# Embedding inputs of a two-block network: loaded and split ahead of the mixer instead of behind it

## The chip, the cores and the metric

One core of one Trainium2 chip runs the whole program, launched once. The metric is the device time in microseconds, the median of 3 runs. Engines: PE is TensorE (matmuls), DVE is VectorE, ACT is ScalarE, POOL is GpSimd, SP is SyncE (here it issues the DMAs of the weights). All arithmetic is float32; matmuls are made of three passes over halves, as told below.

## The reference

Two blocks over 256 tokens of width 1024. The first block is attention (differential and latent) and an FFN. The second has two layers, and the change lies in these. Layer `i` computes, with `rmsnorm` before and after each part:

```
for i in range(2):
    h = h + 0.5 * rmsnorm(ffn(rmsnorm(h)))                 # FFN (i, 0)
    m = retention(rmsnorm(h)) if i == 0 else stick_breaking(rmsnorm(h))
    h = h + rmsnorm(m)                                     # the mixer
    h = h + 0.5 * rmsnorm(ffn(rmsnorm(h)))                 # FFN (i, 1)
    gate = sigmoid(rmsnorm(h) @ ple_w_gate[i])
    e = p[i] @ ple_w_proj[i]                               # the embedding
    h = h + rmsnorm(gate * e)
```

`p[i]` is an input of 256 x 256, `ple_w_proj[i]` one of 256 x 1024. So `e` depends on nothing that is computed before it.

## The kernel before

**Three passes.** Each float32 operand is split into a high half, rounded to the matmul's format (`hi`), and the rest (`lo = x - hi`). A product is `hi*hi + hi*lo + lo*hi`, three matmuls into one PSUM bank (`mm3`). A split is one operation of ACT (the rounding copy) and one of DVE (the subtraction): L180 and L181 for weights (`w_hi`, `w_lo`), L275 and L276 for other tiles (`split`), L408 and L409 for the features of a stage (`x_hi`, `x_lo`).

**Weights.** All weights lie in one array in the order of use. `chunk` loads up to 2048 columns of it by a DMA on SP into one of 3 raw buffers, and splits them in pieces of 512 columns into tiles of the pools `hip` (tag "a") and `lop` (tag "b"), 12 buffers each. Buffers of a tag are given out in the order of the program.

**Stages.** In a stage by tokens (`tokens`), the 256 tokens are two halves `b`, and weights are taken in groups of k-tiles; within a group first half 0, then half 1. At the end of an FFN or mixer `end_stage` runs the output projection (behind a mixer only its second 512 columns, with a last group of 8 k-tiles of 512 columns), and `residual` normalizes each half and adds it to `h`: two squares on ACT with a sum (L377), products on DVE (L387), a power on POOL (L303), and the addition on DVE (L394). `features` prepares a half of `h` for the next stage: 8 transposes on PE (L404) into two PSUM tiles of the pool `psa` (4 banks), 8 `x_hi` and 8 `x_lo`, two more squares for the scale `R`. The squares write to scratch tiles of tag "sq" in the pool `tmp`, 2 buffers, which nobody reads.

**The embedding.** `embed` is called behind the mixer. It opens with a DMA from POOL of `p[i]`, transposed, into `pt` (L1184), in a pool of its own that lies where the mixer's tiles were. It splits `pt` into `pe_a` and `pe_b`, a buffer each of `hip` and `lop` (L1185 to L1189). Then 24 matmuls of 512 columns through `tokens`, with one chunk of weights (4 pieces), fill the four banks of `psa`, and four copies on ACT write `e` (L1194). `ple` uses `e` some 200 us later.

**Order.** The order of each engine's instructions is made by a planner when the program is built. It gives an engine, of the instructions whose inputs and buffers are ready by its own cost model, the one that stands first in the program; `urgent` moves `residual` and `features` up by 100 places. Each engine then works through its list in order, and waits at an instruction whose inputs are late. Tiles of pools that are open at different times share memory, and a tile waits until those that lay there before it are done with.

Of the kernel before, what the change touches and what calls it, by code (L numbers as in the profile page):

```python
# [10 lines left out]
F32 = mybir.dt.float32  # L11
F32R = mybir.dt.float32r
# [6 lines left out]
P = 128  # L19
T = 256  # L20
# [16 lines left out]
SUB = 512  # L37
# [100 lines left out]
class Build:  # L138
# [1038 lines left out]
                self.end_stage("sb_w_out_2", (0,), oT, KT, row, first=first)  # L1177


    def embed(self, emb, i, e):  # L1180

        nc = self.nc
        pt = emb.tile([P, 2, T], F32, name="pt")
        nc.gpsimd.dma_start(pt, self.aps["pT"][:, i * 2 * T : (i + 1) * 2 * T].rearrange("p (k t) -> p k t", k=2))  # L1184
        hi, lo = [  # L1185
            pool.tile([P, SUB], F32R, name=f"pe_{tag}", tag=tag).rearrange("p (k t) -> p k t", k=2)
            for pool, tag in ((self.hip, "a"), (self.lop, "b"))
        ]
        self.split(pt, hi, lo)  # L1189
        parts = [("ple_w_proj_2", (i,), range(j * 512, (j + 1) * 512)) for j in range(2)]  # L1190
        banks = self.banks(self.psa, "a")
        for b, _ in self.tokens(parts, (hi, lo), 2, banks, [[0, 1]]):
            for j in range(2):
                nc.scalar.copy(e[:, b, j * 512 : (j + 1) * 512], banks[b][j])  # L1194
# [30 lines left out]
    def run(self):  # L1225
        tc = self.tc
        self.setup()
        g2 = lambda i, n: self.vec(V_G2 + (i * 8 + n) * 8, 8)
        row = lambda i, n: R_G2 + 4 * i + n // 2
        stage = self.first()  # L1230
        with tc.tile_pool(name="big0", bufs=1) as self.big:
            self.ffn(*stage, ("w_ffn_gate", "w_ffn_up", "w_ffn_down"), (0,), R_FFN, 1.0)
        names = ("ffn_w_gate_2", "ffn_w_up_2", "ffn_w_down_2")
        out = self.aps["out"].rearrange("p (b d) -> p b d", b=2)
        for i in range(2):
            with tc.tile_pool(name=f"big{i}a", bufs=1) as self.big:
                self.ffn(*self.next_stage(g2(i, 0)), names, (i, 0), row(i, 1), 4.0)
            mixer = self.stick if i else self.retention
            mixer(*self.next_stage(g2(i, 2)), row(i, 3))
            with tc.tile_pool(name=f"emb{i}", bufs=1) as emb:  # L1240
                e = emb.tile([P, 2, D], F32, name="e")
                self.embed(emb, i, e)
                with tc.tile_pool(name=f"big{i}b", bufs=1) as self.big:
                    self.ffn(*self.next_stage(g2(i, 4)), names, (i, 1), row(i, 5), 4.0)
                self.ple(i, *self.next_stage(g2(i, 6), 4.0), e, row(i, 7), out if i else None)
        assert self.at == WCOLS * P, (self.at, WCOLS * P)
# [67 lines left out]
```

## Time and profile before

| What | Value |
|---|---|
| time, median of 3 runs | 1652.93 us (1652.63 to 1652.97) |
| the profiled execution | 1655.98 us, span 1654.2 us |
| PE busy | 1617.8 us, 98% of the span |
| DVE, ACT, POOL busy | 65%, 54%, 4% |
| mean granted clock of PE | 0.991 of full speed |
| HBM read | 284.75 MB, 173 GB/s over the span |

Times in the profile count from the start of the span. Busy is the time in which an engine works on an instruction; matmuls overlap, so the start of one to the start of the next tells their pace better than a duration. In a timeline a bracket behind a row is the time that the engine stood idle before it, and what ended that. The granted clock is the share of TensorE's full clock that it got: 1.00 is 2.4 GHz, 0.50 is 1.2 GHz. The first FFN of the second block ends at 686, retention at 887, the stick-breaking mixer at 1417.5.

### The profile page before, as it was taken

To read this page: it belongs to the slowest core of one execution; us is meant where nothing else is said; L and a number is where in the kernel's file an instruction comes from. 1 tells how busy PE (TensorE), PEld (TensorE's weight loads), DVE (VectorE), ACT (ScalarE), POOL (GpSimd) and SP (SyncE) were. 2 spreads that over 40 slices of the span, in tenths; PEclk is the share of its full clock that TensorE was granted. 3 is DMA by queue.
4 is the path that set the end of the run, shared out by engine and by line. 5 is a ranking of instruction groups with operands and counts; after the bars stand their busy time and mean duration, and the time that the engine had idled before them with its cause. 6 is when DMAs were issued, how large, how long until landed. Compare 5 with 4: busy or idle time off the path is not lost. (4 is left out here: it accounts for less than half of the span.)

```text
span 1654.2 us, 23505 instructions
## 1 busy us (share of the span) xinstructions
PE 1617.8 (98%) x8804; PEld 1384.0 (84%) x8804; DVE 1078.4 (65%) x1983; ACT 900.2 (54%) x1789; POOL 69.8 (4%) x107
## 2 busy tenths in 40 slices
PE   7999999999999999999998999999999999899997
PEld 7899889888878888799986888877888799688886
DVE  7887667755557555777765656477655677656546
ACT  6545545655556554645545555476554665655545
POOL 3000000100000000100000000010000100000001
PEclk9999999999999999999999999999999999999999
DMA  7444434555546555444453555555455443355551
GB/s 253 166 140 142 185 103 165 197 200 187 188 159 217 181 179 198 161 178 170 168 185 130 202 202 173 185 191 202 178 179 196 174 176 134 133 190 185 187 181 61
DMA packets 45746, 288.76 MB, mean 175 GB/s; under 512 B 5648, under 2 KB 7440, under 8 KB 12736
## 3 DMA queue, kind: packets, MB, share of 16 engines
q1 hardware_dynamic: 43440, 279.17, 48.2%
q0 software_dynamic: 2192, 8.10, 1.5%
q8 instruction: 69, 1.13, 0.3%
q14 instruction: 45, 0.37, 0.1%
HBM read 284.75 MB, written 1.05 MB: 173 GB/s over the span
## 5 line engine op out<-in xcount | busy, mean ns | idle before, releaser
L181 DVE TENSOR_TENSOR w_lo<-w_raw,w_hi 128x512 fp32r<-128x512 f32 x1054 | 713.3, 690 | 359.4 <-ACT w_hi L180 355.6
L180 ACT CAST w_hi<-w_raw 128x512 fp32r<-128x512 f32 x1054 | 639.8, 620 | 502.1 <-PE ps L189 327.5
L189 PE MATMUL ps<-w_hi,x_hi 128*128 128x512 f32 (+1 forms) x1152 | 438.6, 381 | 0.3 <-ACT x_hi L408 0.2
L189 PE MATMUL ps<-w_lo,x_hi 128*128 128x512 f32 (+1 forms) x1152 | 432.2, 375 | 0.0
L189 PE MATMUL ps<-w_hi,x_lo 128*128 128x512 f32 (+1 forms) x1152 | 432.0, 376 | 0.2
L189 PEld LDWEIGHTS ps<-w_hi,x_lo 128*128 128x128 f32 x1152 | 216.8, 188 | 41.0 <-DVE x_lo L409 1.3
L189 PEld LDWEIGHTS ps<-w_hi,x_hi 128*128 128x128 f32 x1152 | 216.9, 188 | 40.7 <-ACT x_hi L408 3.7
L189 PEld LDWEIGHTS ps<-w_lo,x_hi 128*128 128x128 f32 x1152 | 217.2, 189 | 36.6
L206 PE MATMUL ps<-x_hi,w_hi 128*128 128x256 f32 x696 | 182.8, 290 | 6.8 <-ACT w_hi L180 6.8
L206 PE MATMUL ps<-x_hi,w_lo 128*128 128x256 f32 x696 | 180.0, 286 | 0.1
L189 PE MATMUL ps<-w_hi,a_hi 128*128 128x512 f32 x440 | 174.4, 396 | 0.0
L189 PE MATMUL ps<-w_hi,a_lo 128*128 128x512 f32 x440 | 174.0, 396 | 0.0
L189 PE MATMUL ps<-w_lo,a_hi 128*128 128x512 f32 x440 | 174.0, 395 | 0.0
L206 PEld LDWEIGHTS ps<-x_hi,w_hi 128*128 128x128 f32 x696 | 135.1, 194 | 7.4 <-ACT w_hi L180 6.7
L206 PEld LDWEIGHTS ps<-x_hi,w_lo 128*128 128x128 f32 x696 | 135.1, 194 | 1.1 <-DVE w_lo L181 0.6
L206 PE MATMUL ps<-x_lo,w_hi 128*128 128x256 f32 x696 | 124.3, 285 | 0.0
L206 PEld LDWEIGHTS ps<-x_lo,w_hi 128*128 128x128 f32 x696 | 102.4, 194 | 0.0
L189 PEld LDWEIGHTS ps<-w_hi,a_lo 128*128 128x128 f32 x440 | 82.9, 188 | 19.1
L189 PEld LDWEIGHTS ps<-w_lo,a_hi 128*128 128x128 f32 x440 | 82.9, 188 | 18.8
L189 PEld LDWEIGHTS ps<-w_hi,a_hi 128*128 128x128 f32 x440 | 82.9, 188 | 18.6
L303 POOL TENSOR_TENSOR r<-v,mhalf 128x1 f32<-128x1 f32 (+1 forms) x49 | 38.2, 779 | 1275.9 <-DVE v L367 1134.6
L570 DVE SCALAR_TENSOR_TENSOR a<-ps,R,s 128x512 f32<-128x512 f32 (+1 forms) x60 | 42.2, 703 | 49.8 <-PE ps L189 43.9
(284 smaller groups left out, 1550.5 us busy)
## 6 DMA issues: line engine op xcount, KB each, us to landing
w_raw<-in_w SPq DMA_DIRECT2D x256, 1024.0 KB, 4.9
gr<-in_rows POOLq DMA_DIRECT2D x10, 512.0 KB, 4.8
w_raw<-in_w SPq DMA_DIRECT2D x12, 256.0 KB, 5.4
w_raw<-in_w SPq DMA_DIRECT2D x6, 384.0 KB, 3.1
w_raw<-in_w SPq DMA_DIRECT2D x3, 512.0 KB, 3.2
h<-in_x POOLq DMA_DIRECT2D x1, 1024.0 KB, 7.4
out<-h SPq DMA_DIRECT2D x4, 256.0 KB, 2.6
h<-in_xT SPq DMA_DIRECT2D x3, 256.0 KB, 5.8
```

Source lines behind the costliest of these rows:

```text
L180: nc.scalar.copy(hi[:, :m], r[:, c0:c1])
L181: nc.vector.tensor_sub(lo[:, :m], r[:, c0:c1], hi[:, :m].bitcast(F32))
L189: mm = lambda a, b, **k: nc.tensor.matmul(ps, a, b, skip_group_check=True, **k)
L206: mm = lambda *a, **k: self.nc.tensor.matmul(*a, skip_group_check=True, **k)
L303: self.nc.gpsimd.tensor_tensor(r, v, self.mhalf[:, :n], op=ALU.pow)
L570: nc.vector.scalar_tensor_tensor(a, banks[1], R[:, b : b + 1], s, op0=ALU.mult, op1=ALU.mult)
```

## The change

The DMA of `pt` and its split move to a function of their own, `embed_in`, which `run` calls between the FFN (i, 0) and the mixer. `pt` takes a buffer of tag "sq" in the pool `tmp`. The halves are two tiles of a new pool, `p_halves`, which is opened ahead of the loop and stays open (4 KB of each partition); both layers use the same two. `embed` keeps the matmuls and the copies. The pool `emb` holds `e` alone.

```
-    def embed(self, emb, i, e):
-
-        nc = self.nc
-        pt = emb.tile([P, 2, T], F32, name="pt")
-        nc.gpsimd.dma_start(pt, self.aps["pT"][:, i * 2 * T : (i + 1) * 2 * T].rearrange("p (k t) -> p k t", k=2))
-        hi, lo = [
-            pool.tile([P, SUB], F32R, name=f"pe_{tag}", tag=tag).rearrange("p (k t) -> p k t", k=2)
-            for pool, tag in ((self.hip, "a"), (self.lop, "b"))
-        ]
-        self.split(pt, hi, lo)
+    def embed_in(self, i):
+
+        pt = self.tmp.tile([P, SUB], F32, name="pt", tag="sq")
+        self.nc.gpsimd.dma_start(pt, self.aps["pT"][:, i * 2 * T : (i + 1) * 2 * T])
+        self.split(pt, *self.pe)
+
+    def embed(self, i, e):
+
+        nc = self.nc
+        hi, lo = [t.rearrange("p (k t) -> p k t", k=2) for t in self.pe]
         parts = [("ple_w_proj_2", (i,), range(j * 512, (j + 1) * 512)) for j in range(2)]
...
+        p_halves = self.ctx.enter_context(tc.tile_pool(name="p_halves", bufs=1))
+        self.pe = [p_halves.tile([P, SUB], F32R, name=f"pe_{x}") for x in "hl"]
         for i in range(2):
             with tc.tile_pool(name=f"big{i}a", bufs=1) as self.big:
                 self.ffn(*self.next_stage(g2(i, 0)), names, (i, 0), row(i, 1), 4.0)
+            self.embed_in(i)
             mixer = self.stick if i else self.retention
             mixer(*self.next_stage(g2(i, 2)), row(i, 3))
             with tc.tile_pool(name=f"emb{i}", bufs=1) as emb:
                 e = emb.tile([P, 2, D], F32, name="e")
-                self.embed(emb, i, e)
+                self.embed(i, e)
```

## Rows read from the trace of the kernel before

**Rows 1.** The page's busy time of each engine.

```profile
PE 1617.8 (98%) x8804; PEld 1384.0 (84%) x8804; DVE 1078.4 (65%) x1983; ACT 900.2 (54%) x1789; POOL 69.8 (4%) x107
```

**Rows 2.** Waits of PE, whole run: releaser, us in total, times, longest.

```profile
PE ps L189 <- ACT w_hi L180: 10.0, 2, 5.0
```

**Rows 3.** Timeline of PE at retention's exit: start us, duration us, instruction.

```profile
886.32 0.39 PE L189 MATMUL ps<-w_hi,u_h 128*128 128x512 f32 x1
...
886.78 0.40 PE L189 MATMUL ps<-w_hi,u_l 128*128 128x512 f32 x1
892.17 0.80 PE L189 MATMUL ps<-w_hi,pe_a 128*128 128x512 f32 x1 [5.00 <-ACT w_hi L180]
...
898.97 1.47 PE L404 MATMUL xt<-kc,h 128*128 128x128 f32 x12
900.20 0.48 PE L189 MATMUL ps<-w_lo,pe_a 128*128 128x512 f32 x1
...
901.44 0.39 PE L189 MATMUL ps<-w_hi,x_hi 128*128 128x512 f32 x1
```

**Rows 4.** Stretches at retention's exit: busy by engine, granted clock, DMA share, GB/s.

```profile
894.00:896.00 2.00, 2.00 (x6) 1.57 (x6) 2.00 (x4) 1.91 (x5) 0.48 (x2) 0.50 0.00 0
...
898.00:900.00 2.00, 2.00 (x15) 1.75 (x15) 1.07 (x2) 1.74 (x5) 0.00 (x0) 1.00 0.98 397
```

**Rows 5.** Timeline of PE at the stick-breaking mixer's exit.

```profile
1417.31 0.40 PE L189 MATMUL ps<-w_hi,o_l 128*128 128x512 f32 x1
1422.67 0.80 PE L189 MATMUL ps<-w_hi,pe_a 128*128 128x512 f32 x1 [4.96 <-ACT w_hi L180]
...
1432.87 0.39 PE L189 MATMUL ps<-w_hi,x_hi 128*128 128x512 f32 x1
```

**Rows 6.** Timeline of the other engines at retention's exit.

```profile
881.61 0.60 ACT L377 ACTIVATE sq<-ps 128x512 f32<-128x512 f32 x1 [10.58 <-PE ps L189]
...
887.74 0.59 POOL L1184 DMA_DIRECT2D pt<-in_pT  x1 [3.94 <-PE ps L189]
...
889.51 1.42 DVE L394 SCALAR_TENSOR_TENSOR h<-og,r,h 128x512 f32<-128x512 f32 x2 [0.70 <-POOL r L303]
...
890.98 0.62 ACT L275 CAST pe_a<-pt 128x512 fp32r<-128x512 f32 x1
891.51 1.13 ACT L180 CAST w_hi<-w_raw 128x512 fp32r<-128x512 f32 x2
```

**Rows 7.** DMA issues: engine, count, KB each, median us from issue to landing.

```profile
pt<-in_pT POOLq DMA_DIRECT2D x2, 256.0 KB, 3.2
...
ks<-in_ks POOLq DMA_DIRECT2D x1, 192.0 KB, 4.7
```

**Rows 8.** A stretch ahead of retention's exit, columns as in rows 4.

```profile
878.00:880.00 2.00, 2.00 (x10) 1.61 (x9) 0.00 (x0) 0.00 (x0) 0.00 (x0) 1.00 0.00 0
```

**Rows 9.** Waits of PE at both entries: 676 to 700, then 1296 to 1318.

```profile
PE xt L404 <- DVE h L394: 1.2, 2, 0.7
...
PE xt L404 <- DVE h L394: 0.7, 2, 0.5
```

**Rows 10.** Users of tile `ta`: duration ns min/median/max, first and last start us.

```profile
L925 DVE TENSOR_TENSOR mt<-t,ta x8: 418/418/422, 271.7 to 284.1; 128x256 f32<-128x256 f32 x8
...
L508 DVE TENSOR_SCALAR ta<-pos,kc x2: 335/350/365, 19.0 to 284.4; 128x256 f32<-128x256 int32 x2
```

**Rows 11.** Timeline of ACT at retention's entry.

```profile
685.88 0.61 ACT L377 ACTIVATE sq<-ps 128x512 f32<-128x512 f32 x1
...
687.57 0.65 ACT L377 ACTIVATE sq<-h 128x512 f32<-128x512 f32 x1
...
690.52 0.87 ACT L408 ACTIVATE x_hi<-xt,vecs 128x128 fp32r<-128x128 f32 x3
```

**Rows 12.** Timeline of PE at retention's entry.

```profile
693.34 0.39 PE L189 MATMUL ps<-w_hi,x_hi 128*128 128x512 f32 x1
```

**Rows 13.** Waits at the stick-breaking mixer's entry, 1300 to 1318.

```profile
DVE tri_r L499 <- DMA ks<-in_ks: 0.8, 1, 0.8
```

## The prediction

> **What bounds the kernel now.** I read the page's engine totals first, then the waits of TensorE (PE), then the timeline where these waits lie, then the engine that ends each. PE is busy 98% of the span [rows 1], so only two things shorten the run: PE waiting less, or PE running the same matmuls faster. The waits of PE for the whole run name their largest group at once: 10.0 us in two waits of 5.0, matmuls of L189 waiting for a `w_hi` cast on ScalarE (ACT) [rows 2]. Both are the first matmul of `embed`, one behind each mixer.
>
> At retention's exit the last matmul of the output projection starts at 886.78 and, at the pace of the two before it (0.23 us each, from 886.32), leaves PE at 887.01. The first embedding matmul starts at 892.17: 5.16 us of nothing. From there to the first matmul of the next FFN at 901.44, PE does 24 embedding matmuls and 12 transposes [rows 3]. At the pace of the rows around it that is 24 x 0.233 = 5.59 us, and the 12 transposes took 1.23 us (898.97 to 900.20), 6.82 in all; it took 9.27. The rest is the clock: the granted clock was 0.50, the lower level (1.2 GHz), in 894 to 896, and 1.00 (2.4 GHz) again in 898 to 900 [rows 4]; PE had stood idle before it fell. So this exit costs 901.44 - 887.01 - 6.82 = 7.61 us more than its work. At the exit of the stick-breaking mixer the same rows are 1417.31 (end 1417.54), 1422.67 and 1432.87 [rows 5]: 15.33 - 6.82 = 8.51 us. Together 16.12 us.
>
> **What ends the gap.** ACT's queue. `pt`'s tile lies where the mixer's tiles were, so its DMA leaves at 887.74, behind the last matmul; it lands 3.2 us later, `pe_a` is cast at 890.98, and only then come the casts of the embedding's weights at 891.51 [rows 6, 7]. These weights waited for no data: nothing moved on the DMA queues in 878 to 880, so the three raw buffers were full [rows 8], and ACT had stood idle 10.58 us before 881.61 [rows 6]. They stood behind `pe_a` because both take buffers of tag "a" of the same pool in program order.
>
> **The change, part by part.** The instructions are the same: two DMAs, two casts, two subtractions. Nothing is saved in work; six instructions move, and `pe` leaves the weights' pools.
>
> *Exit.* `pe` is ready some 200 us (retention) or 110 us (stick) early. The last group of the output projection holds 8 of the 12 buffers (8 k-tiles of 512 columns), so 4 are free, and the embedding's weights are exactly 4 pieces (2 x 1024 columns in 512s). ACT and VectorE (DVE) can split them in the 10.58 us that they idle, and the embedding's matmuls follow the projection without a gap; PE then has no reason to lose its clock. Gain between 0 and 16.12 us; I take all of it, less what is late next. That is: the embedding takes all four banks of its PSUM pool, so the transposes of the next stage wait for a copy of `e`; and the second half of `h` is written at 889.51 + 1.42 = 890.93 [rows 6], a chain that doesn't move. With the embedding from 887.01, 24 matmuls and 8 transposes end at 893.4, and the first FFN group needs the first half's tiles alone, so `h` is in time. For the copies I take the size of PE's waits before such transposes elsewhere, 0.5 us per exit, between 0 and 1.2 [rows 9]: 1.0 us in all. `e`'s own memory is free with the last matmul, ahead of its first copy.
>
> *Entry.* `pt` is now one of the two "sq" buffers, which go round in program order: the planner reaches far ahead (retention's angle table was started at 284.4, 400 us early) but not past an earlier user of the tag (behind the last `mt` at 284.1) [rows 10]. So `pt` is not loaded hundreds of us ahead; its buffer follows the squares of the FFN's end, and the DMA leaves POOL behind these, at the latest with the end of the last one, 685.88 + 0.61 = 686.5 [rows 11]. Cast (0.62) and subtraction (0.69) then stand in the queues of ACT and DVE at the mixer's entry, where features and weight casts are dense. Behind the cast wait `x_hi` tiles; PE waits for these. Lower bound: the new order may remove PE's waits for `h` there, 1.2 and 0.7 us [rows 9], so -1.2. Upper bound: the second feature square (687.57) needs `pt`'s buffer back. `pt` lands at 686.5 + 4.7 = 691.2, the longer of the two landings in [rows 7], cast and subtraction end at 692.5, ACT is 4.9 us late; `x_hi` of the second half, started at 690.52, was used from 693.34 [rows 11, 12], 2.8 us of cover: PE loses 2.1. The nearest row is `ks`, a POOL DMA of just this place at the other entry: DVE stood 0.8 us for it [rows 13], and PE lost nothing but its usual 0.7 for `h`. I take 0.4 us per entry, 0.8 in all. POOL's issue (0.59) stands ahead of the power that `h` waits for; if it falls on it, it is up to 0.59, inside these bounds. Without its cover the cast costs PE 0.62.
>
> A POOL DMA landed in 3.2 us at an exit, where DVE has gaps, and in 4.7 at an entry, where it is busy [rows 7]; sizes and addresses differ too, so the two rows bound `pt`'s landing and don't say why. The Trainium skill has a rule against this move: by "SBUF — State Buffer", section "SBUF: two separate sides", the descriptors of a DMA from POOL cannot be written while DVE runs an operation in a two-port mode, some 620 ns against 3100 ns there. By these figures `pt` would land 2.5 us later than 3.2, after 5.7, an entry would cost 3.1 at worst, and the sum would be 16.1 - 1.0 - 6.2 = 8.9, some 1644 us: an estimate from that page, and rival 1 below by a worse road.
>
> *Pools.* `p_halves` adds 4 KB under all later pools. Stages meet in other addresses by it; tiles there are reused many us apart, so I take 0, with the 0.5 of one more transposes' wait as its price [rows 9].
>
> **Sum.** 16.12 - 1.0 - 0.8 = 14.3 us. Against the profiled execution (1655.98 us, span 1654.2) that is 1641.7; the median of the runs shown, 1652.93, lies 3.05 below the profiled time, so 1652.93 - 14.3 = 1638.6 us.
>
> **Rivals.**
> 1. The entry pays in full: ACT is held for `pt` at both entries, 2.1 us each. For it: the saturated queues and the shared "sq" buffers; against: a planner that places the cast when it reckons the data there, and the `ks` row. 16.12 - 1.0 - 4.2 = 10.9, so 1642.0.
> 2. The gap moves behind the embedding: its matmuls start at once, but the next FFN waits for features, and PE idles (and loses its clock) there. For it: `h` of the second half comes from the same fixed chain. Against: that chain ends at 890.93, ahead of 893.4. If the whole gap came back, only the entries' 0.8 would be left: 1653.7, no change.
> 3. Slower: the weights' casts stay where they are in ACT's order, behind the squares of the second half, since nothing forces the planner to take the free buffers early. The first cast then merely takes `pe_a`'s place at 890.98, 0.53 us earlier; twice 1.1. The entries pay 2.1 each, and POOL's issue delays `h` by 0.59 each: -1.1 + 4.2 + 1.2 = +4.3, so 1657.2. It decides as soon as an entry loses more than 0.53. Against: the 10.58 us of idle ACT; and a planner that started the angle table as soon as its tag was free [rows 10].
> That the change doesn't do what it says (`pt` not ahead of the mixer) would be rival 3 without its entry costs, about 1652.
>
> **How the numbers follow.** Forecast 0.77, rival 1 0.11, rival 2 0.07, rival 3 0.05. The predicted time is the forecast's, 1638.6. Its own ends are 16.12 + 2 x 1.2 = 18.5 (1634.4), all bounds at their best, and 16.12 - 2 x 1.2 - 2 x 2.1 = 9.5 (1643.4), all at their worst, which takes in rival 1; with 0.5 for the addresses and 0.59 for each POOL issue, 1.7, the range is 1634.4 to 1645.1. It leaves out rivals 2 and 3. About 0.2% (3.3 us) is what a measurement of this kernel can tell from no change. Faster: forecast and rival 1, 0.88; same: rival 2, 0.07; slower: rival 3, 0.05.
>
> **What would show it.** Exit: no wait of PE for `w_hi` at L189 among its waits, four `w_hi` casts before 881, granted clock 1.00 through both exits, and some 6.8 to 8 us from the projection's last matmul to the FFN's first. Entry: `pt` issued on POOL within some 6 us ahead of 687, and at the same point of the stick mixer's entry; PE's waits in both entries within 1 us of [rows 9]. I am wrong if a PE wait of over 2 us stands at any of the four places, or if the exits keep a stretch at 0.50.

## The result, and the profile after

The changed kernel takes 1642.86 us (median of 4 runs, 1641.67 to 1645.08) against 1652.95: a ratio of 0.9933, 95% interval 0.9921 to 0.9945, faster by more than the 0.2% that can be told. The profiled execution took 1643.92 us, span 1642.2, 12.0 less than the span before. On TensorE's timeline these 12.0 us fall into stretches so (a stretch runs from the start of its first matmul to the start of the next stretch's first, us):

| Stretch | before | after | difference |
|---|---|---|---|
| start to retention's entry (first transpose at 682.07, 682.91) | 682.07 | 682.91 | +0.84 |
| retention's entry, to its first L206 | 16.71 | 16.74 | +0.03 |
| its body, to the projection's last matmul | 188.00 | 187.86 | -0.14 |
| its exit, to the FFN's first matmul | 14.66 | 7.68 | -6.98 |
| to the stick-breaking mixer's entry | 401.53 | 401.55 | +0.02 |
| that entry | 26.98 | 28.70 | +1.72 |
| that body | 87.36 | 87.73 | +0.37 |
| that exit | 15.56 | 7.63 | -7.93 |
| the rest | | | +0.1 |

The page's busy line, answering to [rows 1]:

```profile
PE 1613.3 (98%) x8804; PEld 1380.9 (84%) x8804; DVE 1078.7 (66%) x1983; ACT 901.4 (55%) x1789; POOL 70.6 (4%) x107
```

The instructions are as many as before; PE is busy 4.5 us less, which fits the 4.0 us that are put down to its clock below. The waits of PE in the whole run (releaser, total us, times, longest):

```profile
PE ps L206 <- ACT w_hi L180: 7.2, 1, 7.2
...
PE xt L404 <- ACT e L1194: 0.8, 2, 0.4
PE ps L189 <- ACT x_hi L408: 0.7, 3, 0.3
PE o L649 <- ACT zs L1141: 0.6, 2, 0.4
```

The 10.0 us of [rows 2] are gone. In their place stand the wait for the copies of `e`, 0.4 per exit, and two small ones, for `x_hi` (0.7, of which 0.5 at the stick-breaking entry) and for a second `zs`, to which I come back. PE at retention's exit, answering to [rows 3], then at the stick-breaking one, to [rows 5]:

```profile
887.51 0.39 PE L189 MATMUL ps<-w_hi,u_l 128*128 128x512 f32 x1
887.74 0.39 PE L189 MATMUL ps<-w_hi,pe_h 128*128 128x512 f32 x1
...
894.78 0.66 PE L404 MATMUL xt<-kc,h 128*128 128x128 f32 x4 [0.42 <-ACT e L1194]
895.19 0.48 PE L189 MATMUL ps<-w_hi,x_hi 128*128 128x512 f32 x1
...
1413.17 0.40 PE L189 MATMUL ps<-w_hi,o_l 128*128 128x512 f32 x1
1413.41 0.39 PE L189 MATMUL ps<-w_hi,pe_h 128*128 128x512 f32 x1
...
1420.38 0.66 PE L404 MATMUL xt<-kc,h 128*128 128x128 f32 x4 [0.38 <-ACT e L1194]
```

The embedding starts 0.23 us behind the projection's last matmul, and the FFN 7.45 us later (the other FFN starts at 1420.80, 7.39 us later). Two stretches of retention's exit, columns as in [rows 4] (the third number from the end is the granted clock):

```profile
888.00:890.00 2.00, 2.00 (x10) 1.65 (x9) 2.00 (x4) 2.00 (x7) 0.00 (x0) 1.00 0.00 0
...
894.00:896.00 2.00, 1.57 (x10) 1.09 (x9) 2.00 (x7) 2.00 (x7) 0.55 (x1) 1.00 0.34 66
```

The clock stays at its higher level, where [rows 4] had 0.50. ACT ahead of the exit, answering to [rows 6] and [rows 8]:

```profile
874.69 2.71 ACT L180 CAST w_hi<-w_raw 128x512 fp32r<-128x512 f32 x4 [2.86 <-PE ps L189]
882.37 0.60 ACT L377 ACTIVATE sq<-ps 128x512 f32<-128x512 f32 x1 [4.96 <-PE ps L189]
...
883.52 4.34 ACT L180 CAST w_hi<-w_raw 128x512 fp32r<-128x512 f32 x7
```

Four weights' casts stand in the time that ACT idled before, and seven more ahead of the exit; nothing waits there for `pt`. What the change costs is seen at the stick-breaking entry, on POOL, ACT and PE:

```profile
1300.93 0.59 POOL L1079 DMA_DIRECT2D ks<-in_ks  x1 [5.12 <-ACT w_hi L180]
1301.52 0.54 POOL L1183 DMA_DIRECT2D pt<-in_pT  x1
...
1303.04 0.66 ACT L377 ACTIVATE sq<-h 128x512 f32<-128x512 f32 x1
...
1306.24 0.62 ACT L275 CAST pe_h<-pt 128x512 fp32r<-128x512 f32 x1 [2.46 <-DMA pt<-in_pT]
1306.77 0.36 ACT L408 ACTIVATE x_hi<-xt,vecs 128x128 fp32r<-128x128 f32 x1
...
1306.89 0.39 PE L189 MATMUL ps<-w_hi,x_lo 128*128 128x512 f32 x1
1307.18 0.50 PE L189 MATMUL ps<-w_hi,x_hi 128*128 128x512 f32 x1
...
1308.58 0.50 PE L189 MATMUL ps<-w_hi,x_hi 128*128 128x512 f32 x1 [0.17 <-ACT x_hi L408]
...
1311.01 0.50 PE L189 MATMUL ps<-w_hi,x_hi 128*128 128x512 f32 x1 [0.34 <-ACT x_hi L408]
1311.34 0.39 PE L189 MATMUL ps<-w_lo,x_hi 128*128 128x512 f32 x1
```

POOL waits for an ACT cast with the DMA of `ks` at the head of its list; `pt` leaves behind it, ACT stands 2.46 us for it, and every `x_hi` behind that is late. The waits view gives PE only 0.5 us of this. The starts give more: the 11 steps from the start at 1306.89 to that at 1311.34 take 4.45 us instead of 11 x 0.23 = 2.53, so 1.9. The wait of `ks` is as long in the kernel before, where no `pt` stood behind it:

```profile
1307.17 0.59 POOL L1079 DMA_DIRECT2D ks<-in_ks  x1 [5.13 <-ACT w_hi L180]
```

At retention's entry `pt` left at 683.27 and landed 3.3 us later, and its cast, which stands further back in ACT's list there, waited for nothing:

```profile
692.14 0.63 ACT L275 CAST pe_h<-pt 128x512 fp32r<-128x512 f32 x1
```

### The profile page after: what moved, and what is told of

Its sections match the earlier page's. It is cut to its first block, busy times and chain, and to the rows that moved or that the text cites. A ratio compares the mean times of both kernels' runs of the same rounds, so it can differ in the third digit from the quotient of the medians.

```text
span 1642.2 us, 23512 instructions
## 1 busy us (share of the span) xinstructions
PE 1613.3 (98%) x8804; PEld 1380.9 (84%) x8804; DVE 1078.7 (66%) x1983; ACT 901.4 (55%) x1789; POOL 70.6 (4%) x107
## 4 chain that ended last, share of the span: by engine, by line
PE 42%; issue 12%; DVE 2%; ACT 1%; POOL 1%; DMA 0%; DVEq 0%; POOLq 0%; ACTq 0%
PE ps L189 31%; PE ps L206 8%; PE at L575 1%; PE o L189 1%; POOL r L303 1%; PE xt L404 0%; DVE w_lo L181 0%; DVE h L394 0%; ACT sq L377 0%; PE S L1113 0%; PE S L993 0%; ACT w_hi L180 0%; DMA pt<-in_pT 0%; DVE og L387 0%; PE o L649 0%
## 5 line engine op out<-in xcount | busy, mean ns | idle before, releaser
L189 PE MATMUL ps<-w_hi,x_hi 128*128 128x512 f32 (+1 forms) x1152 | 439.3, 382 | 1.0 <-ACT x_hi L408 0.7
L189 PE MATMUL ps<-w_lo,x_hi 128*128 128x512 f32 (+1 forms) x1152 | 432.1, 375 | 0.0
L189 PE MATMUL ps<-w_hi,x_lo 128*128 128x512 f32 (+1 forms) x1152 | 431.7, 376 | 0.2
L189 PEld LDWEIGHTS ps<-w_hi,x_hi 128*128 128x128 f32 x1152 | 217.0, 188 | 42.2 <-ACT x_hi L408 5.6
L189 PEld LDWEIGHTS ps<-w_hi,x_lo 128*128 128x128 f32 x1152 | 216.8, 188 | 41.3 <-DVE x_lo L409 1.5
L189 PEld LDWEIGHTS ps<-w_lo,x_hi 128*128 128x128 f32 x1152 | 217.2, 189 | 36.5
L206 PE MATMUL ps<-x_hi,w_hi 128*128 128x256 f32 x696 | 182.7, 290 | 7.2 <-ACT w_hi L180 7.2
L206 PE MATMUL ps<-x_hi,w_lo 128*128 128x256 f32 x696 | 179.9, 286 | 0.4 <-DVE w_lo L181 0.3
L189 PE MATMUL ps<-w_hi,a_hi 128*128 128x512 f32 x440 | 174.4, 396 | 0.0
L189 PE MATMUL ps<-w_hi,a_lo 128*128 128x512 f32 x440 | 174.0, 396 | 0.0
L189 PE MATMUL ps<-w_lo,a_hi 128*128 128x512 f32 x440 | 174.0, 395 | 0.0
L206 PEld LDWEIGHTS ps<-x_hi,w_hi 128*128 128x128 f32 x696 | 134.8, 194 | 7.9 <-ACT w_hi L180 7.2
L206 PEld LDWEIGHTS ps<-x_hi,w_lo 128*128 128x128 f32 x696 | 134.8, 194 | 1.8 <-DVE w_lo L181 1.3
L206 PE MATMUL ps<-x_lo,w_hi 128*128 128x256 f32 x696 | 124.1, 285 | 0.0
L206 PEld LDWEIGHTS ps<-x_lo,w_hi 128*128 128x128 f32 x696 | 102.0, 194 | 0.0
L189 PEld LDWEIGHTS ps<-w_hi,a_lo 128*128 128x128 f32 x440 | 82.9, 188 | 19.2
L189 PEld LDWEIGHTS ps<-w_hi,a_hi 128*128 128x128 f32 x440 | 82.9, 188 | 18.7
L189 PEld LDWEIGHTS ps<-w_lo,a_hi 128*128 128x128 f32 x440 | 82.9, 189 | 18.6
```

The source lines that it names most:

```text
L189: mm = lambda a, b, **k: nc.tensor.matmul(ps, a, b, skip_group_check=True, **k)
L206: mm = lambda *a, **k: self.nc.tensor.matmul(*a, skip_group_check=True, **k)
```

## The experiments

Each ratio is to the kernel before, run on the same chip. The first is the changed kernel again.

> The changed kernel once more, for its spread and a second trace. Theory: the two exits give 6.98 and 7.93 us again in this trace, and the entry of the stick-breaking mixer (from the first four transposes of `features` to the first matmul of L206) again takes near 28.7 us instead of 26.98, with ACT waiting some 2.5 us for `pt` ahead of the cast `pe_h`. Median 1641 to 1645. Rival (the lost 2 us at that entry is chance of one execution): the entry comes back to 27.0.

Measured: 1644.11 us, ratio 0.9931 (0.9919 to 0.9944); kernel before 1655.12 (15 runs). The exits take 7.66 and 7.63 us, the entries 16.75 and 28.68, the stick-breaking body 87.71. These rows are the kernel's own. The time ahead of retention's entry moves between executions, 679.89 to 682.91 us over all twelve traces: in the three traces below 680.4 the granted clock stays at 1.00 from 204 to 208, in each of the nine others it is down to between 0.50 and 0.57 in one of the two stretches of 2 us there.

**`ks` out of the way.** `ks` is loaded once, ahead of the loop:

```
-            ks = sp.tile([P, NKS], F32, name="ks")
-            nc.gpsimd.dma_start(ks, self.aps["ks"])
+            ks = self.ks
...
+        self.ks = p_halves.tile([P, NKS], F32, name="ks")
+        self.nc.gpsimd.dma_start(self.ks, self.aps["ks"])
         for i in range(2):
```

> The changed kernel with `ks` (the constants of the stick-breaking mixer) loaded once, into a tile of `p_halves`, ahead of the loop, so that its DMA no longer stands ahead of `pt`'s in POOL's list at that entry. Theory (the 1.7 us lost there are ACT's wait for `pt`, and `pt` is late because POOL's list holds `ks` ahead of it, which waits for a `w_hi` cast until 1300.9): `pt` is issued some 4 us earlier, within 1 us of the end of the square of the second half's first 512 columns; ACT's wait of 2.46 us is gone, the entry takes 27.0 to 27.5, the median is 1.2 to 1.8 us lower, near 1641. Rival W (the cast and the subtraction themselves cost it, in full queues): the entry stays above 28.3. Rival P (a DMA from POOL lands late where DVE is busy): `pt` is issued early and still takes 4.7 us to land; it then lands at the same distance from the issue but ahead of the cast, so the time falls as well, and only the landing tells.

Measured: 1640.46 us, 0.9913 (0.9899 to 0.9927). The entry takes 26.71 us: all of the 1.7 us is back (I had expected 27.0 to 27.5). POOL and ACT there:

```profile
1294.75 0.59 POOL L1182 DMA_DIRECT2D pt<-in_pT  x1 [1.29 <-ACT sq L377]
...
1301.27 0.64 ACT L275 CAST pe_h<-pt 128x512 fp32r<-128x512 f32 x1
```

The cast and the subtraction are still there and the entry is as short as before the change, so it was the wait that cost the 1.7 us. The landing fell from 4.7 to 2.9 us. DMA issues in the two entries (KB each, us to landing), after and then with `ks` early:

```profile
w_raw<-in_w SPq DMA_DIRECT2D x1, 1024.0 KB, 4.9
...
pt<-in_pT POOLq DMA_DIRECT2D x1, 256.0 KB, 4.7
ks<-in_ks POOLq DMA_DIRECT2D x1, 192.0 KB, 4.7
```

```profile
w_raw<-in_w SPq DMA_DIRECT2D x1, 1024.0 KB, 4.8
pt<-in_pT POOLq DMA_DIRECT2D x1, 256.0 KB, 2.9
```

After, SP had issued a megabyte of weights at 1300.25, and `pt` at 1301.52 fell into it; with `ks` early `pt` had landed (1294.75 + 2.9) before the weights were issued at 1297.89. DVE being busy doesn't explain it: while `pt` landed in 2.9 us, DVE was busy all the time (third of the busy columns), and while it took 4.7, DVE stood idle in part:

```profile
1295.00:1296.00 1.00, 1.00 (x9) 0.89 (x8) 1.00 (x2) 0.64 (x3) 0.34 (x1) 1.00 0.00 0
1296.00:1297.00 1.00, 1.00 (x6) 0.82 (x5) 1.00 (x4) 0.95 (x3) 0.00 (x0) 1.00 0.73 254
1297.00:1298.00 1.00, 1.00 (x6) 0.82 (x5) 1.00 (x3) 1.00 (x4) 0.00 (x0) 1.00 0.02 8
```

```profile
1302.00:1303.00 1.00, 1.00 (x6) 0.82 (x5) 0.58 (x3) 1.00 (x4) 0.62 (x2) 1.00 0.83 336
...
1305.00:1306.00 1.00, 1.00 (x6) 0.79 (x6) 0.00 (x0) 0.00 (x0) 0.83 (x3) 1.00 0.76 261
```

**`pt` in a buffer of its own.** `pt` comes from the new pool instead of tag "sq", and `embed_in` is called ahead of the FFN (i, 0):

```
-        pt = self.tmp.tile([P, SUB], F32, name="pt", tag="sq")
+        pt = self.p_halves.tile([P, SUB], F32, name="pt")
...
+            self.embed_in(i)
             with tc.tile_pool(name=f"big{i}a", bufs=1) as self.big:
...
-            self.embed_in(i)
```

> The changed kernel with `pt` in a tile of its own in `p_halves` instead of a buffer of tag sq, and loaded and split ahead of the FFN (i, 0), a stage earlier still. Theory: no engine waits for `pt` at any entry, both entries cost what they cost before the change (26.98 us at the stick-breaking mixer), exits as in the changed kernel (some 7.5 us from the projection's last matmul to the FFN's first). 1.5 to 2.5 us below the changed kernel, near 1641. Rival W: as the cast and subtraction move to where ACT and DVE have holes, this one is faster too, but then the kernel with only `ks` moved is not. If neither is faster, the loss at the entry was chance.

Measured: 1641.94 us, 0.9915 (0.9901 to 0.9928); the stick-breaking entry takes 26.89 us. So two different ways of having `pt` early each remove the loss, one of them with `ks` left at its place. The rows of `pt`:

```profile
L1183 POOL DMA_DIRECT2D pt<-in_pT x2: 590/591/592, 497.3 to 504.3; - x2
...
DMA to landing us min/median/max: 2.9/4.1/5.3
```

The first of these DMAs, at 497.3, follows SP's weights of 496.62 and has no other POOL DMA ahead of it; it is the 5.3 (its cast starts at 502.62). So a landing can be long with no other POOL DMA ahead. What both long landings have is weights issued just ahead of `pt`; both also have another POOL DMA, `gr`, issued 3.0 and 3.6 us behind it, which these rows don't exclude.

**Halves of their own, loaded behind the mixer.** The two new tiles stay, `embed_in` is called where `embed` was, `pt` again in the pool `emb`:

```
-        pt = self.tmp.tile([P, SUB], F32, name="pt", tag="sq")
+        pt = emb.tile([P, SUB], F32, name="pt")
...
-            self.embed_in(i)
...
+                self.embed_in(i, emb)
                 self.embed(i, e)
```

> The kernel before with one part of the change: the halves of the embedding's input have tiles of their own (not buffers of the weights' tags), but `pt` is loaded and split behind the mixer, in memory that the mixer held, as before. Theory (the gap at the exits ends with `pt`'s landing): the weights are split early, but the first embedding matmul still waits for `pe_h`, until 891.6 in the times of the kernel before instead of 892.17; PE idles 4.5 us, the clock falls, and only the weight casts' share comes back: 1 to 3 us in all, 1650 to 1652. Rival (what held the exits was the order of the weights' buffers behind `pe`, not the load): the exits close, 1641 to 1645.

Measured: 1654.22 us, 0.9994 (0.9985 to 1.0003). PE's largest wait and the start of the embedding:

```profile
PE ps L189 <- ACT pe_h L275: 9.3, 2, 4.8
```

```profile
884.61 0.40 PE L189 MATMUL ps<-w_hi,u_l 128*128 128x512 f32 x1
889.55 0.80 PE L189 MATMUL ps<-w_hi,pe_h 128*128 128x512 f32 x1 [4.54 <-ACT pe_h L275]
```

The weights are split early (seven casts from 880.60) and 0.7 us of the two gaps goes, 10.0 to 9.3; the rest now waits for `pe_h` itself. The 0.7 us is less than the 1 to 3 us that I expected, and the time can't be told from that of the kernel before. Own buffers free the weights, but it takes the early load to make the gain. Whether the early load would do without buffers of its own, no run tells.

**The clock's share.** To price the clock apart from the gap, matmuls of the identity with itself fill the gap in the kernel before:

```
+        idle = self.psa.tile([P, 512], F32, name="idle", tag="a")
+        for _ in range(40):
+            nc.tensor.matmul(idle[:, 0:P], self.ident, self.ident, start=True, stop=True)
```

> The kernel before with 40 added matmuls of the identity with itself (128 columns each), written into a tile that nobody reads, ahead of the embedding's matmuls of both layers: the wait for the weights stays, but TensorE has work at the start of it. My theory says that an exit of before loses two things, the wait itself (5.2 us) and then the clock (2.45 us at retention's exit, 3.38 us at the stick-breaking one, the stretch behind the wait less 6.82 us of work). Then here the start of the embedding stays within 0.5 us of where it was (some 5.1 us behind the projection's last matmul), the clock that falls behind it is later or does not fall, and of the 5.8 us that the clock took some 4.3 to 5.8 come back: ratio 0.9965 to 0.9975. The rival: the stretch behind the wait is set by the splits of the embedding's weights, which come one by one at the pace of ACT and DVE, not by the clock. Then it stays 9.3 and 10.2 us long, and the time is that of before within 0.1%.

Measured: 1656.04 us, 1.0016 (1.0007 to 1.0025), slower. I had reckoned half of their time:

```profile
885.33 9.09 PE L1192 MATMUL idle<-kc 128*128 128x128 f32 x80
894.17 0.48 PE L189 MATMUL ps<-w_hi,pe_a 128*128 128x512 f32 x1
...
901.09 0.39 PE L189 MATMUL ps<-w_hi,x_hi 128*128 128x512 f32 x1
```

The profile has two records for each of the 40, 80 of 0.11 us, which outlast the gap by 3.7 us (894.17 - 885.09 against 892.17 - 886.78). The clock stayed at 1.00 and the stretch behind shrank from 9.27 to 6.92 us, but the weights had time to be split meanwhile, so the rival was not excluded. Hence 23 of them, the length of the gap:

> The kernel before with 23 added identity matmuls instead of 40, in the same place: at the 0.11 us of one of their 46 passes in a3_busy_gap they take 5.1 us, just the wait, so the embedding starts where it did (5.4 us behind the start of the projection's last matmul, within 0.3), and its weights are split as late as in the kernel before. If the clock is what makes the stretch behind the wait 9.3 and 10.4 us long, it is 7.0 to 7.6 us here with a granted clock of 1.00, and the ratio is 0.996 to 0.998. If the weights' splits pace it, the stretch stays over 9 us at whatever clock and the time is that of before.

Measured: 1652.15 us, 0.9984 (0.9975 to 0.9993).

```profile
887.00 5.29 PE L1192 MATMUL idle<-kc 128*128 128x128 f32 x46
892.20 0.49 PE L189 MATMUL ps<-w_hi,pe_a 128*128 128x512 f32 x1
893.00 0.50 PE L189 MATMUL ps<-w_lo,pe_a 128*128 128x512 f32 x1 [0.31 <-DVE w_lo L181]
...
899.92 0.39 PE L189 MATMUL ps<-w_hi,x_hi 128*128 128x512 f32 x1
```

```profile
892.00:894.00 2.00, 1.69 (x8) 0.92 (x7) 1.84 (x5) 2.00 (x6) 0.63 (x2) 1.00 0.00 0
```

The embedding starts where it did, and its stretch is 7.72 us instead of 9.27; at the other exit 7.71 (1421.43 to 1429.14) instead of 10.20. So the clock is a share of its own, in these two traces 1.55 + 2.49 = 4.0 us. The stretches are a little longer than the 7.0 to 7.6 us that I expected, and the ratio lies just outside 0.996 to 0.998. I had counted all that was over 6.82 us as clock; part of it is late weights, as the wait for `w_lo` shows. And the share differs between executions: the last kernel below, which has the exits of the kernel before, has stretches of 9.42 and 8.68 us, by which the clock is 1.70 + 0.97 = 2.7 us. At its second exit the granted clock is 0.79 in 1426 to 1428, where the kernel before has 0.50. The ratio of 0.9984 is 2.6 us, by its interval 1.2 to 4.1.

**How steady before is.** The kernel before again, for its trace.

> The kernel before again, for a second trace of it: it tells how far its rows vary between executions. If they are the kernel's own, the retention's exit takes 14.7 us from the projection's last matmul to the FFN's first, the stick-breaking one 15.6, both within 1 us, the entry of the stick-breaking mixer 27.0 within 0.2, and the body of that mixer 87.4 within 0.1. If the 0.37 us that this body is longer in every kernel with halves of their own is only a difference of executions, it is 87.7 here.

Measured: exits 14.63 and 15.54 us, entry 27.08, body 87.32; one run, 1656.15. The three traces with the exits of before (this one, the first, and the last one below) took 14.63 to 14.79 us at retention's exit, but 14.17 to 15.56 at the other. So up to 1.4 us of the 7.93 gained there may belong to the execution.

**`ks` early, and a try at the rest.**

> The changed kernel with ks loaded once ahead of the loop, a second time, beside the kernel before on this chip: 0.9913 again within 0.0013 if the 3 us that it was ahead of the changed kernel alone are its own; 0.993 if they were the spread of executions. Its entry at the stick-breaking mixer takes 26.7 us again by the one, and by both its exits 7.6 us each.

Measured: 1639.17 us, 0.9913 (0.9900 to 0.9926), entry 26.70, exits 7.64 and 7.62. This is the fastest measured, though the kernel with `pt` in a buffer of its own (0.9915) can't be told from it. Its gain over the changed kernel is 2.0 us in the traces (28.68 to 26.70). The ratios (0.9931 against 0.9913) say 3 us, but their intervals overlap by a little, and the time ahead of retention, which moves between executions, is in them.

The copies of `e` then go half to DVE, to see whether ACT's list keeps PE waiting for them:

```
-                nc.scalar.copy(e[:, b, j * 512 : (j + 1) * 512], banks[b][j])
+                copy = nc.vector.tensor_copy if j else nc.scalar.copy
+                copy(e[:, b, j * 512 : (j + 1) * 512], banks[b][j])
```

> The kernel of a3_ks_again, with the copies of the second half of the embedding's columns out of PSUM on DVE instead of ACT: two queues empty the banks that the next stage's transposes wait for. If the 0.4 us that TensorE waits there per exit is ACT's queue, the waits go under 0.1 and the time falls by 0.4 to 0.8 us (ratio 0.0002 to 0.0005 below its neighbour's, less than a comparison of medians tells; the waits in the trace tell it). If it is the end of the last matmul itself, or DVE is late there with the features, the waits stay or move to x_hi, and the time is the same or up to 0.8 us longer.

Measured: 1642.12 us, 0.9930 (0.9917 to 0.9942). PE's wait is no shorter:

```profile
PE xt L404 <- DVE e L1194: 1.1, 2, 0.5
```

A copy took 0.68 us on DVE against 0.59 on ACT; the exits are 7.89 and 7.87, 0.25 longer each. At retention's exit the copy that PE waits for starts at 892.74 on DVE, right behind the addition of `h` (891.41, 1.41 us). So one list was put in place of another, and what made PE wait in ACT's stays open. The times are 3 us above those of the kernel beside it, which the traces don't show: their spans, 1640.4 and 1639.6, are 0.8 apart.

**The body's 0.37 us.** The kernel before with the new pool, its two tiles set to zero once on POOL and not used:

```
+        p_halves = self.ctx.enter_context(tc.tile_pool(name="p_halves", bufs=1))
+        self.pe = [p_halves.tile([P, SUB], F32R, name=f"pe_{x}") for x in "hl"]
+        self.nc.gpsimd.memset(self.pe[0].bitcast(F32), 0.0)
+        self.nc.gpsimd.memset(self.pe[1].bitcast(F32), 0.0)
```

> The kernel before with the two 2 KB tiles of the changed kernel's new pool in the same place (set to zero once, and not used), so that all later tiles lie where they lie in the changed kernel, with the order of before. If the 0.37 us that the stick-breaking body lost comes from the embedding's weights, which are now split in it (a subtraction ahead of the last product of zs on DVE), it is 87.3 here, with one wait of PE for zs. If it comes from addresses, it is 87.7 with two waits.

Measured: body 87.32 us, one wait for `zs` of 0.4; one run, 1655.25. So addresses don't make the 0.37 us. DVE at the last head of this mixer, after (with PE behind it), then in this kernel:

```profile
1398.30 0.69 DVE L181 TENSOR_TENSOR w_lo<-w_raw,w_hi 128x512 fp32r<-128x512 f32 x1 [0.70 <-ACT w_hi L180]
1398.90 0.55 DVE L1140 TENSOR_TENSOR zs<-zs,c 128x384 f32<-128x384 f32 x1
...
1400.06 0.70 PE L649 MATMUL o<-zs,v 128*128 128x256 f32 x2 [0.16 <-ACT zs L1141]
```

```profile
1403.71 0.56 DVE L1140 TENSOR_TENSOR zs<-zs,c 128x384 f32<-128x384 f32 x1 [2.61 <-PE c L1139]
```

A subtraction of the embedding's weights, split early, stands ahead of the product that PE needs, which without it starts as soon as `c` is there. By the starts PE's step to L649 is 0.56 us (1399.50 to 1400.06), in this kernel 0.23 (1404.72 to 1404.95). All kernels with halves of their own have this (87.70 to 87.73), those without don't (87.32 to 87.36): some 0.37 us is the price of the early weights.

## Why the prediction was right, and where it was not

**Exits: right.** 16.12 - 1.0 = 15.1 us was forecast, 14.9 came (6.98 + 7.93). All its signs are there: no wait for `w_hi` at L189, four casts before 881, clock 1.00, 7.45 and 7.39 us of stretch, 0.42 and 0.38 for `e` against the 0.5 assumed. By the filled gap the 14.9 of these traces divide into 10.3 of wait (5.16 + 5.13), 4.0 of clock, and 0.6 of weights that came late (7.72 + 7.71 - 7.45 - 7.39). The prediction's "The rest is the clock" was too much by about 1.8 of 5.8 (2.45 + 3.38): 0.6 are the late weights, and 1.2 are what 7.45 and 7.39 lie over 6.82, against which the sum had set its 1.0. So the sum took no harm. Rival 2 fell: no new gap behind the embedding. Rival 3 fell: the planner did take the free buffers early.

**Entries: one right, one mis-sized.** The mis-sized term is "I take 0.4 us per entry, 0.8 in all": 0.03 at retention, 1.72 at the stick-breaking mixer, under the bound of 2.1. I worked the entry out on retention's rows and carried it to the other. At retention itself the bound's road was not taken: the square of `h` that I had wait for `pt`'s buffer ran without a wait, with the three others between 687.80 and 691.40, all ahead of the cast. At the other entry the `ks` of [rows 13], which I used as a price, was in truth the instruction ahead of `pt` in POOL's list, and it waits 5.12 us for ACT; its 5.13 us in the trace of before could have told me. So `pt` left 0.6 us behind it, fell into the weights' DMA, and the planner's place for the cast came 2.46 us too early. Rival 1 was thus right at one entry and wrong at the other; that its 1642.0 lies nearest the measured time is no proof of it, as it priced both at 2.1. The sign that I had named, PE's waits within 1 us of [rows 9], came true and didn't show the loss: the waits view has 0.5 us of it.

**The landing.** I left open why [rows 7] have 3.2 and 4.7 us, and set a DVE with gaps against a busy one. In these rows' own trace DVE was busy 2.30 of the 4 us from 887 and 3.47 of the 5 us from 1307, so the two places differ little in it. The rule of the Trainium skill that I weighed ("SBUF — State Buffer", section "SBUF: two separate sides") would have operations of DVE in a two-port mode delay the DMA. I priced it without asking whether DVE's operations at the entry are in such a mode, and no trace here shows it, so the rule is neither borne out nor refuted. The runs show that this DVE work (`h`, `w_lo`, `og`, `x_lo`) didn't hold the DMA up: 2.9 us with DVE fully busy. Over all twelve traces the landings of `pt` and `ks` that took 4.5 to 5.3 us had a weights' DMA issued 0.7 to 1.3 us ahead, and those of 2.9 to 3.5 had none in the 7.6 us ahead. Weights issued 0.5 us behind `pt`, as where `pt` was loaded late, left it at 3.3 and 3.5. No run changed the weights' DMA alone, so this is a reading, not a test.

**Not foreseen.** 0.37 us in the stick-breaking body, which I had no term for: the weights that ACT and DVE split early meet the last head there. 0.84 us ahead of retention, where nothing was moved: a difference of executions.

**From span to median.** Against the profiled execution the sum gave 1641.7 and 1643.92 came; the 2.2 are made of +0.95 entries, +0.84 head, +0.37 - 0.14 bodies, +0.2 exits. The predicted 1638.6 was another 3.05 lower, as I took the three runs of 1652.93 for the kernel's usual time. Of 44 later runs of the kernel before, with a median of 1654.0, 10 lay below 1652.93 and 8 above 1655.98: the three runs were on its low side and the profiled execution on its high side. The measured 1642.86 lies 4.3 above the predicted time; it is inside the range because the range had both entries at their worst.

## What to carry to other kernels

When a load is moved ahead, read the in-order list of the engine that issues it at every place it moves to: what stands ahead there, and what that waits for. A price taken from one place doesn't hold for its twin. And when a gap is closed on an engine whose clock falls after idling, count the wait and the slow stretch behind it as two terms, and the work that fills the gap as load for its neighbours.

## What the runs showed of the hardware

An idle of 5.2 us on TensorE cost 1.55 and 2.49 us more behind it, at the lower clock, in one trace, and 1.70 and 0.97 in another with the same exits; identity matmuls that nobody reads, put in the same place, kept the clock at 1.00 and made the kernel 0.16% faster (0.9984, 0.9975 to 0.9993). A 256 KB DMA from POOL landed in 2.9 to 3.5 us at most places, and in 4.7 and 5.3 where a megabyte of weights had been issued 1.3 and 0.7 us ahead. The issue of `ks` on POOL, which waited 5.12 us, held the one behind it: `pt` left 4.78 us behind the start of the entry's first transpose, and 0.36 us behind it with `ks` loaded early.
